# Instance norm over 512 rows: tiles of 48 KiB per partition in four slots, with parts of 16 KiB at both ends

## The chip, the core and the metric

The kernel runs on one core of one Trainium2 chip. The metric is device time in microseconds (us), from several runs of the whole program; before the change the median of 6 runs is 1248.16 us (1247.94 to 1249.8). One further run was recorded by the hardware profiler. PE is the matrix engine, DVE the vector engine, ACT the scalar engine, POOL the general engine that here only sets constants up, SP the engine that issues the loads. 16 DMA engines move data between HBM and the on-chip memory (128 partitions).

## What is computed

```python
def reference(x, eps):              # x: (8, 64, 32, 64, 64) float32
    mean = np.mean(x, axis=(2, 3, 4), keepdims=True)
    var = np.var(x, axis=(2, 3, 4), keepdims=True)
    return ((x - mean) / np.sqrt(var + eps)).astype(np.float32)
```

There are 8 x 64 = 512 instances of 32 x 64 x 64 = 131,072 floats. The input has 268.4 MB and the output as much; each is moved once.

## The kernel before

**Tiles and slots.** A tile is 128 partitions x 8,192 floats (32 KiB per partition, 4 MiB): 8 whole instances, each spread over 16 partitions. There are 64 tiles and six slots for them; tile k lives in slot k mod 6. Tiles 0 to 59 run in a loop of 10 rounds with six slots each (lines 168 to 173), tiles 60 to 62 behind it, and tile 63 as two halves of 4,096 columns side by side in one slot (lines 157 to 160), with lanes of their own. A lane is one set of semaphores and small columns.

**One tile.** ACT and DVE each sum half of the columns (lines 107 and 79). A matmul with a block-diagonal matrix holding 1/131072 (`avg`, line 136) adds up the 16 partitions of each instance, and DVE adds the two halves into the negative mean (line 82). ACT takes the square of x minus the mean over the whole tile with a running sum (line 113), a second matmul joins the partitions (line 143), ACT takes the root (line 120), and DVE the reciprocal and the shift (lines 89 and 92). Then ACT scales one half of the columns in place (line 123) and DVE the other (line 95).

**Queues.** SP issues all loads in order (lines 178 to 194): the first six at once, each later one when the store of the tile that last had its slot is complete (`stored`). ACT issues the stores (line 130) behind its own scaling, when both scalings are `done`. Both queues feed the same 16 DMA engines, 8 partitions of a transfer on each. Every engine works through the tiles in order, so the next tile's sums on ACT stand behind this tile's store. POOL prepares `avg` and `eps_t` (lines 196 to 215); PE and ACT wait for it once. ACT waits at the end for all stores.

Of the kernel before, what the change touches and what calls it, by code (L numbers as in the profile page):

```python
# [9 lines left out]
def kernel(  # L10
# [6 lines left out]
    nc = tc.nc  # L17
# [4 lines left out]
    P = 128  # L22
# [5 lines left out]
    COLS = 8192  # L28
    SLOTS = 6
    FULL = P * COLS // n_elem  # L30
    n_tiles = n_inst // FULL
    ROUNDS = (n_tiles - 1) // SLOTS
    LANES = SLOTS + 2

    x_f = x.rearrange("b c d h w -> (b c) (d h w)")
    out_f = out.rearrange("b c d h w -> (b c) (d h w)")
    x_t = x_f.rearrange("(k i) (s f) -> k (i s) f", i=FULL, s=P // FULL)
    out_t = out_f.rearrange("(k i) (s f) -> k (i s) f", i=FULL, s=P // FULL)
    x_h = x_f.rearrange("(k i) (s f) -> k (i s) f", i=FULL // 2, s=2 * P // FULL)
    out_h = out_f.rearrange("(k i) (s f) -> k (i s) f", i=FULL // 2, s=2 * P // FULL)  # L40

    ctx.enter_context(tc.tile_critical(name="norm"))  # L42

    def sbuf(name, shape, dtype=fp32):
# [4 lines left out]
    unused = sbuf("unused", [P, COLS], mybir.dt.uint8)  # L49
    eps_t = sbuf("eps_t", [P, 1])  # L50
    avg = {n: sbuf(f"avg{n}", [P, P]) for n in (FULL, FULL // 2)}
    small = [sbuf(f"small{i}", [P, 8]) for i in range(LANES)]
    psum = [
        ctx.enter_context(nc.psum_tensor(f"psum{i}", [P, 512], fp32))
        for i in range(LANES)
    ]

    def semaphores(name, n):
        return [ctx.enter_context(nc.semaphore(f"{name}{i}")) for i in range(n)]

    ready = semaphores("ready", 1)[0]
    landed = semaphores("landed", LANES)
    summed = semaphores("summed", LANES)
    meaned = semaphores("meaned", LANES)
    centred = semaphores("centred", LANES)
    squared = semaphores("squared", LANES)
    varied = semaphores("varied", LANES)
    rooted = semaphores("rooted", LANES)
    scaled = semaphores("scaled", LANES)
    shifted = semaphores("shifted", LANES)  # L70
    done = semaphores("done", LANES)
    stored = semaphores("stored", LANES)
# [3 lines left out]
    def on_vector(eng, t, lane, n, c1, c2, c16):  # L76
        w = t.shape[1] // 2
        a = small[lane]
        eng.reduce_sum(  # L79
            out=a[:, 0:1], in_=t[:, :w], axis=mybir.AxisListType.X  # L80
        )._wait_ge(landed[lane], c16).then_inc(summed[lane], 1)
        eng.tensor_reduce(  # L82
            out=a[:, 2:3],
            in_=psum[lane][:, 0:2],
            axis=mybir.AxisListType.X,
            op=Alu.add,
            negate=True,
        )._wait_ge(meaned[lane], c1).then_inc(centred[lane], 1)
        eng.reciprocal(out=a[:, 5:6], in_=a[:, 4:5])._wait_ge(  # L89
            rooted[lane], c1  # L90
        ).then_inc(scaled[lane], 1)
        eng.tensor_mul(out=a[:, 6:7], in0=a[:, 2:3], in1=a[:, 5:6])._wait_ge(  # L92
            scaled[lane], c1
        ).then_inc(shifted[lane], 1)
        eng.tensor_scalar(  # L95
            out=t[:, w:],
            in0=t[:, w:],
            scalar1=a[:, 5:6],
            scalar2=a[:, 6:7],
            op0=Alu.mult,  # L100
            op1=Alu.add,
        )._wait_ge(shifted[lane], c1).then_inc(done[lane], 1)

    def on_scalar(eng, t, lane, n, c1, c2, c16, dst):
        w = t.shape[1] // 2
        a = small[lane]
        eng.activation(  # L107
            out=unused[:, w : 2 * w],
            in_=t[:, w:],
            func=Act.Identity,  # L110
            accum_out=a[:, 1:2],
        )._wait_ge(landed[lane], c16).then_inc(summed[lane], 1)
        eng.activation(  # L113
            out=unused[:, : 2 * w],
# [4 lines left out]
        )._wait_ge(centred[lane], c1).then_inc(squared[lane], 1)  # L119
        eng.activation(  # L120
            out=a[:, 4:5], in_=psum[lane][:, 2:3], func=Act.Sqrt, bias=eps_t[:, 0:1]
        )._wait_ge(varied[lane], c1).then_inc(rooted[lane], 1)
# [4 lines left out]
            scale=a[:, 5:6],  # L127
            bias=a[:, 6:7],
        )._wait_ge(shifted[lane], c1).then_inc(done[lane], 1)
        eng.dma_start(out=dst, in_=t)._wait_ge(done[lane], c2).then_inc(  # L130
# [3 lines left out]
    def on_tensor(eng, t, lane, n, c1, c2, c16):  # L134
        a = small[lane]
        eng.matmul(  # L136
            out=psum[lane][:, 0:2],
            lhsT=avg[n][:],
            rhs=a[:, 0:2],
            start=True,  # L140
            stop=True,
        )._wait_ge(summed[lane], c2).then_inc(meaned[lane], 1)
        eng.matmul(  # L143
            out=psum[lane][:, 2:3],
            lhsT=avg[n][:],
            rhs=a[:, 3:4],
            start=True,
            stop=True,
        )._wait_ge(squared[lane], c1).then_inc(varied[lane], 1)


    rest = [
        (x_t[k], out_t[k], slots[k % SLOTS][:], k % SLOTS, k // SLOTS + 1, FULL)
        for k in range(ROUNDS * SLOTS, n_tiles - 1)
    ]
    last = (n_tiles - 1) % SLOTS
    for h in range(2):
        k = 2 * (n_tiles - 1) + h
        half = slots[last][:, h * COLS // 2 : (h + 1) * COLS // 2]
        rest.append((x_h[k], out_h[k], half, SLOTS + h, 1, FULL // 2))  # L160

    def over_tiles(eng, step, with_target=False):
        counts = [
            ctx.enter_context(eng.register(f"{step.__name__}_c{m}")) for m in (1, 2, 16)
        ]
        for c, m in zip(counts, (1, 2, 16)):
            eng.reg_mov(c, m)
        with eng.Fori(0, ROUNDS) as it:
            for s in range(SLOTS):
                more = (out_t[it * SLOTS + s],) if with_target else ()  # L170
                step(eng, slots[s][:], s, FULL, *counts, *more)
            for c, m in zip(counts, (1, 2, 16)):
                eng.reg_add(c, c, m)
        for _, dst, t, lane, c, n in rest:
            more = (dst,) if with_target else ()
            step(eng, t, lane, n, c, 2 * c, 16 * c, *more)

    def load_all(eng):
        for s in range(SLOTS):
            eng.dma_start(out=slots[s][:], in_=x_t[s]).then_inc(landed[s], 16)  # L180
# [8 lines left out]
        for src, _, t, lane, c, n in rest:  # L189
            behind = lane if lane < SLOTS else last  # L190
            uses = c - 1 if lane < SLOTS else ROUNDS
            eng.dma_start(out=t, in_=src)._wait_ge(stored[behind], 16 * uses).then_inc(
                landed[lane], 16
            )

    def set_up(eng):
        count = 0
        for n, m in avg.items():
            split = P // n

            eng.memset(m[:], 1.0 / n_elem).then_inc(ready, 1)  # L201
            count += 1
            for sign in (-1, 1):
                eng.affine_select(  # L204
                    out=m[:],
                    in_=m[:],
                    pattern=[[sign * split, n], [0, split]],
# [3 lines left out]
                    channel_multiplier=-sign,  # L211
# [53 lines left out]
```

## Time and profile before

| what | value |
|---|---|
| median of 6 runs | 1248.16 us (1247.94 to 1249.8) |
| the profiled execution, its own time | 1247.89 us |
| its span, first to last instruction | 1246.2 us |
| ACT busy | 986.0 us (79%), 410 instructions |
| DVE busy | 467.9 us (38%), 325 instructions |
| PE busy | 76.3 us (6%) |
| DMA | 18,722 packets, 536.90 MB, 431 GB/s over the span |
| loads, 4 MiB each: issue to landing | 53.3 us (median of 63) |
| stores, 4 MiB each: issue to landing | 45.3 us (median of 63) |

The span is what the instructions cover; the time is 1.69 us longer. A packet is one row of one transfer (one partition's contiguous bytes), or the 4-byte write behind each transfer's share on a DMA engine that counts up its semaphore. Busy shares are averages over the whole span.

### The profile page before, as it was taken

The numbers are of one execution on the slowest core, as the hardware profiler recorded it, in microseconds if no ns is written. First come the engines' busy times: TensorE is split into PE (matmuls) and PEld (weight loads), VectorE is DVE, ScalarE is ACT, GpSimd is POOL, SyncE is SP. The second block draws the span as 40 slices with busy tenths as digits, with TensorE's granted clock in tenths as the row PEclk, the third lists the DMA queues.
The fourth block names the chain that finished last, engine by engine and source line by source line (L and its number), as shares of the span: only waits on it lengthen the run. The fifth ranks groups of instructions, "written<-read, shape, count | busy, mean of one in ns | idle before, by whom it ended". The sixth has DMA issues, their size and how long they took to land.

```text
span 1246.2 us, 1808 instructions
## 1 busy us (share of the span) xinstructions
PE 76.3 (6%) x260; PEld 65.2 (5%) x260; DVE 467.9 (38%) x325; ACT 986.0 (79%) x410; POOL 1.9 (0%) x11
## 2 busy tenths in 40 slices
PE   0000000000000000000000000000000000000000
PEld 0000000000000000000000000000000000000000
DVE  2344334433334334343343433434334333343331
ACT  5888888887787878778777877787787778878774
POOL 0000000000000000000000000000000000000000
DMA  9999999999999999999999999999999999999998
GB/s 404 421 438 433 426 438 438 430 428 438 435 429 431 438 435 428 432 436 436 427 433 436 435 428 432 438 434 426 435 438 433 427 435 438 432 426 438 438 429 380
DMA packets 18722, 536.90 MB, mean 431 GB/s; under 512 B 2080, under 2 KB 2080, under 8 KB 2080
## 3 DMA queue, kind: packets, MB, share of 16 engines
q1 hardware_dynamic: 9360, 268.44, 50.0%
q10 hardware_dynamic: 9360, 268.44, 49.9%
q14 instruction: 2, 0.02, 0.0%
HBM read 268.44 MB, written 268.44 MB: 431 GB/s over the span
## 4 chain that ended last, share of the span: by engine, by line
ACT 48%; DVE 29%; another core or an unknown queue 13%; PE 6%; issue 1%; DMA 1%; ACTq 0%; DVEq 0%; SPq 0%
ACT unused L113 37%; DVE small L79 18%; DVE slot L95 8%; ACT slot L123 4%; ACT unused L107 4%; PE psum L136 3%; PE psum L143 3%; ACT small L120 1%; ACT L120 1%; DMA slot<-in_x_dram 1%; DVE small L89 1%; DVE small L82 1%; DVE small L92 1%; ACTq L130 0%
## 5 line engine op out<-in xcount | busy, mean ns | idle before, releaser
L113 ACT ACTIVATE unused<-slot,small 128x8192 uint8<-128x8192 f32 (+1 forms) x65 | 456.1, 7016 | 90.1 <-DVE small L82 90.1
L79 DVE TENSOR_REDUCE small<-slot 128x1 f32<-128x4096 f32 (+1 forms) x65 | 282.9, 4353 | 163.6 <-DMA slot<-in_x_dram 163.6
L107 ACT ACTIVATE unused<-slot 128x4096 uint8<-128x4096 f32 (+1 forms) x65 | 231.7, 3564 | 82.0 <-DMA slot<-in_x_dram 76.8
L123 ACT ACTIVATE slot<-slot,small 128x4096 f32<-128x4096 f32 (+1 forms) x65 | 243.7, 3749 | 27.6 <-DVE small L92 27.6
L89 DVE RECIPROCAL small<-small 128x1 f32<-128x1 f32 x65 | 10.6, 164 | 533.8 <-ACT small L120 533.8
L95 DVE TENSOR_SCALAR slot<-slot,small 128x4096 f32<-128x4096 f32 (+1 forms) x65 | 154.7, 2380 | 2.4
L136 PE MATMUL psum<-small,avg 128*128 128x2 f32 x130 | 38.1, 363 | 674.0 <-DVE small L79 548.5
L136 PEld LDWEIGHTS psum<-small,avg 128*128 128x128 f32 x130 | 32.6, 311 | 679.4 <-DVE small L79 552.8
L143 PE MATMUL psum<-small,avg 128*128 128x1 f32 x130 | 38.2, 363 | 480.5 <-ACT unused L113 480.5
L143 PEld LDWEIGHTS psum<-small,avg 128*128 128x128 f32 x130 | 32.6, 312 | 486.1 <-ACT unused L113 486.1
L120 ACT ACTIVATE small<-psum,eps_t 128x1 f32<-128x1 f32 x65 | 17.0, 261 | 37.3 <-PE psum L143 37.2
L82 DVE TENSOR_REDUCE small<-psum 128x1 f32<-128x2 f32 x65 | 10.3, 159 | 63.0 <-PE psum L136 63.0
L107 ACT ACT_TABLE_LOAD x10 | 12.8, 1283 | 10.4 <-ACT slot L123 7.1
L120 ACT ACT_TABLE_LOAD x10 | 12.8, 1283 | 0.2
L107 ACT ACTIVATION_READ_ACCUMULATOR unused<-slot 128x1 f32 x65 | 12.1, 186 | 0.0
L113 ACT ACTIVATION_READ_ACCUMULATOR unused<-slot,small 128x1 f32 x65 | 12.1, 186 | 0.0
L92 DVE TENSOR_TENSOR small<-small 128x1 f32<-128x1 f32 x65 | 10.3, 159 | 2.2
L204 POOL TENSOR_SCALAR_AFFINE_SELECT avg<-avg 128x128 f32<-128x128 f32 x4 | 1.3, 326 | 0.3
L201 POOL MEMSET avg<- 128x128 f32 x2 | 0.4, 206 | 0.5 <-SPq L42 0.5
L246 POOL MEMSET const-bfloat16-1.0<- 128x1 bf16 x1 | 0.1, 103 | 0.0
L246 POOL MEMSET const-uint8-127<- 128x1 uint8 x1 | 0.1, 102 | 0.0
L246 POOL MEMSET const-float32-0.0<- 128x1 f32 x1 | 0.1, 99 | 0.3 <-issue 0.3
(2 smaller groups left out, 0.2 us busy)
## 6 DMA issues: line engine op xcount, KB each, us to landing
slot<-in_x_dram SPq DMA_DIRECT2D x63, 4096.0 KB, 53.3
out_dram<-slot ACTq DMA_DIRECT2D x63, 4096.0 KB, 45.3
slot<-in_x_dram SPq DMA_DIRECT2D x2, 2048.0 KB, 55.6
out_dram<-slot ACTq DMA_DIRECT2D x2, 2048.0 KB, 14.7
```

The costliest lines, as they stand in the source:

```text
L79: eng.reduce_sum(out=a[:, 0:1], in_=t[:, :w], axis=mybir.AxisListType.X)._wait_ge(landed[lane], c16).then_inc(summed[lane], 1)
L82: eng.tensor_reduce(out=a[:, 2:3], in_=psum[lane][:, 0:2], axis=mybir.AxisListType.X, op=Alu.add, negate=True,)._wait_ge(meaned[lane], c1) ...
L89: eng.reciprocal(out=a[:, 5:6], in_=a[:, 4:5])._wait_ge(rooted[lane], c1).then_inc(scaled[lane], 1)
L92: eng.tensor_mul(out=a[:, 6:7], in0=a[:, 2:3], in1=a[:, 5:6])._wait_ge(scaled[lane], c1).then_inc(shifted[lane], 1)
L95: eng.tensor_scalar(out=t[:, w:], in0=t[:, w:], scalar1=a[:, 5:6], scalar2=a[:, 6:7], op0=Alu.mult, op1=Alu.add,)._wait_ge(shifted[lane], ...
L107: eng.activation(out=unused[:, w : 2 * w], in_=t[:, w:], func=Act.Identity, accum_out=a[:, 1:2],)._wait_ge(landed[lane], c16).then_inc(sum ...
L113: eng.activation(out=unused[:, : 2 * w], in_=t, func=Act.Square, bias=a[:, 2:3], accum_out=a[:, 3:4],)._wait_ge(centred[lane], c1).then_in ...
L120: eng.activation(out=a[:, 4:5], in_=psum[lane][:, 2:3], func=Act.Sqrt, bias=eps_t[:, 0:1])._wait_ge(varied[lane], c1).then_inc(rooted[lane ...
L123: eng.activation(out=t[:, :w], in_=t[:, :w], func=Act.Identity, scale=a[:, 5:6], bias=a[:, 6:7],)._wait_ge(shifted[lane], c1).then_inc(don ...
L136: eng.matmul(out=psum[lane][:, 0:2], lhsT=avg[n][:], rhs=a[:, 0:2], start=True, stop=True,)._wait_ge(summed[lane], c2).then_inc(meaned[lan ...
L143: eng.matmul(out=psum[lane][:, 2:3], lhsT=avg[n][:], rhs=a[:, 3:4], start=True, stop=True,)._wait_ge(squared[lane], c1).then_inc(varied[la ...
L204: eng.affine_select(out=m[:], in_=m[:], pattern=[[sign * split, n], [0, split]], compare_op=Alu.is_ge, fill=0.0, base=0 if sign < 0 else s ...
```

## The change

The data are cut anew, in address order: two parts of 4,096 columns (16 KiB per partition, 2 MiB, 4 instances), then 41 tiles of 12,288 columns (48 KiB per partition, 6 MiB, 12 instances), then three more parts. The whole tiles use four slots and 10 rounds of a loop plus tile 40. The first two parts lie in slots 2 and 3 and have lanes of their own, and the loads of tiles 2 and 3 wait for their stores. The last three parts lie side by side in slot 1, behind the store of tile 37.

A partition's 48 KiB can now hold the end of one instance and the start of the next, but each 16 KiB chunk belongs to one instance. So all sums are kept per chunk, spread with a 0/1 mask (`belongs`) to columns (instance class, chunk), joined by one matmul, added, and picked back per chunk with the mask (`over_instance`, twice per tile). DVE takes the sum of chunk 0 and of the last 1,536 columns, centres chunk 0 in place, takes its squares with a two-input instruction, and scales chunks 0 and 1; ACT takes the other sums, the squares of chunks 1 and 2, and scales chunk 2. The store of tile 40 is no longer issued by ACT: SP issues it on the load queue, behind the loads of the last three parts. SP, not ACT, waits for the last stores. POOL also builds the mask, DVE waits for POOL once, and ACT loads its function table ahead of its first wait.

The functions for the parts (`part_on_vector`, `part_on_scalar`, `part_on_tensor`, `part`) repeat the old steps on 4,096 columns, with constants in their waits. `over_tiles` runs parts 0 and 1, then the loop of 10 rounds, then tile 40 (where ACT gets no target and so issues no store), then parts 2 to 4. `CHUNK` is 4,096, so `n_tiles` is 41, `n_parts` 5 and `ROUNDS` 10.

```diff
-    COLS = 8192
-    SLOTS = 6
+    CHUNK = 4096
+    THIRDS = 3
+    COLS = THIRDS * CHUNK
+    SLOTS = 4
+    PART = P * CHUNK // n_elem
+    FRONT = 2
+    n_tiles = (n_inst // PART - FRONT) // THIRDS - 1
+    n_parts = n_inst // PART - THIRDS * n_tiles
+    ROUNDS = n_tiles // SLOTS
+    LANES = SLOTS + n_parts
...
+    within = sbuf("within", [P, PART * THIRDS, THIRDS])
+    TURN = 1536
+    belongs = sbuf("belongs", [P, THIRDS, THIRDS + 1])
...
+    SUMS, MEANS, SQUARES, VARS, ROOTS, SCALES, SHIFTS = 0, 28, 31, 55, 58, 61, 64
+    AXIS = mybir.AxisListType.X
+    def column(a, first, j):
+        return a[:, first + j : first + j + 1]
+    def block(a, first, n, m):
+        return a[:, first : first + n * m].rearrange("p (n m) -> p n m", m=m)
+    def spread(a, first, m):
+        return a[:, first : first + m].unsqueeze(1).to_broadcast([P, THIRDS, m])
+    def over_instance(eng, a, p, at, m, to, negate, c1, wait, steps):
+        n = THIRDS
+        by_both = at + m
+        by_instance = by_both + n * m
+        by_chunk = by_instance + n
+        eng.tensor_tensor(
+            out=block(a, by_both, n, m),
+            in0=spread(a, at, m),
+            in1=belongs[:, :, :m],
+            op=Alu.mult,
+        )._wait_ge(*wait).then_inc(steps[0], 1)
+        eng.tensor_reduce(
+            out=a[:, by_instance : by_instance + n],
+            in_=p.rearrange("p (n m) -> p n m", m=m),
+            axis=AXIS,
+            op=Alu.add,
+        )._wait_ge(steps[1], c1).then_inc(steps[2], 1)
+        eng.tensor_tensor(
+            out=block(a, by_chunk, n, n),
+            in0=spread(a, by_instance, n),
+            in1=belongs[:, :, :n].rearrange("p i c -> p c i"),
+            op=Alu.mult,
+        )._wait_ge(steps[2], c1).then_inc(steps[3], 1)
+        eng.tensor_reduce(
+            out=a[:, to : to + n],
+            in_=block(a, by_chunk, n, n),
+            axis=AXIS,
+            op=Alu.add,
+            negate=negate,
+        )._wait_ge(steps[3], c1).then_inc(steps[4], 1)
+    def tile_on_vector(eng, t, lane, c1, c3, c4, c16):
+        a, p = small[lane], psum[lane]
+        chunk = [t[:, i * CHUNK : (i + 1) * CHUNK] for i in range(THIRDS)]
+        for j, part in ((0, chunk[0]), (3, t[:, COLS - TURN :])):
+            eng.reduce_sum(out=column(a, SUMS, j), in_=part, axis=AXIS)._wait_ge(
+                landed[lane], c16
+            ).then_inc(summed[lane], 1)
+        over_instance(
+            eng, a, p[:, 0:12], SUMS, 4, MEANS, True, c1, (summed[lane], c4),
+            (sorted_[lane], meaned[lane], joined[lane], picked[lane], centred[lane]),
+        )
+        eng.tensor_scalar(
+            out=chunk[0],
+            in0=chunk[0],
+            scalar1=column(a, MEANS, 0),
+            scalar2=None,
+            op0=Alu.add,
+        )._wait_ge(centred[lane], c1).then_inc(moved[lane], 1)
+        eng.tensor_tensor_reduce(
+            out=unused[2][:],
+            in0=chunk[0],
+            in1=chunk[0],
+            scale=1.0,
+            scalar=0.0,
+            op0=Alu.mult,
+            op1=Alu.add,
+            accum_out=column(a, SQUARES, 0),
+        )._wait_ge(moved[lane], c1).then_inc(squared[lane], 1)
+        over_instance(
+            eng, a, p[:, 12:21], SQUARES, 3, VARS, False, c1, (squared[lane], c3),
+            (sorted2[lane], varied[lane], joined2[lane], picked2[lane], gathered[lane]),
+        )
+        eng.reciprocal(out=a[:, SCALES : SCALES + 3], in_=a[:, ROOTS : ROOTS + 3])._wait_ge(
+            rooted[lane], c1
+        ).then_inc(scaled[lane], 1)
+        eng.tensor_mul(
+            out=a[:, SHIFTS : SHIFTS + 3],
+            in0=a[:, MEANS : MEANS + 3],
+            in1=a[:, SCALES : SCALES + 3],
+        )._wait_ge(scaled[lane], c1).then_inc(shifted[lane], 1)
+        eng.tensor_scalar(
+            out=chunk[0],
+            in0=chunk[0],
+            scalar1=column(a, SCALES, 0),
+            scalar2=None,
+            op0=Alu.mult,
+        )._wait_ge(scaled[lane], c1).then_inc(done[lane], 1)
+        eng.tensor_scalar(
+            out=chunk[1],
+            in0=chunk[1],
+            scalar1=column(a, SCALES, 1),
+            scalar2=column(a, SHIFTS, 1),
+            op0=Alu.mult,
+            op1=Alu.add,
+        )._wait_ge(shifted[lane], c1).then_inc(done[lane], 1)
+    def tile_on_scalar(eng, t, lane, c1, c3, c4, c16, dst):
+        a = small[lane]
+        chunk = [t[:, i * CHUNK : (i + 1) * CHUNK] for i in range(THIRDS)]
+        for j, part in ((1, chunk[1]), (2, chunk[2][:, : CHUNK - TURN])):
+            eng.activation(
+                out=unused[j - 1][:, : part.shape[1]],
+                in_=part,
+                func=Act.Identity,
+                accum_out=column(a, SUMS, j),
+            )._wait_ge(landed[lane], c16).then_inc(summed[lane], 1)
+        for j in (1, 2):
+            eng.activation(
+                out=unused[j - 1][:],
+                in_=chunk[j],
+                func=Act.Square,
+                bias=column(a, MEANS, j),
+                accum_out=column(a, SQUARES, j),
+            )._wait_ge(centred[lane], c1).then_inc(squared[lane], 1)
+        eng.activation(
+            out=a[:, ROOTS : ROOTS + 3],
+            in_=a[:, VARS : VARS + 3],
+            func=Act.Sqrt,
+            bias=eps_t[:, 0:1],
+        )._wait_ge(gathered[lane], c1).then_inc(rooted[lane], 1)
+        eng.activation(
+            out=chunk[2],
+            in_=chunk[2],
+            func=Act.Identity,
+            scale=column(a, SCALES, 2),
+            bias=column(a, SHIFTS, 2),
+        )._wait_ge(shifted[lane], c1).then_inc(done[lane], 1)
+        if dst is not None:
+            eng.dma_start(out=dst, in_=t)._wait_ge(done[lane], c3).then_inc(
+                stored[lane], 16
+            )
+    def tile_on_tensor(eng, t, lane, c1, c3, c4, c16):
+        a, p = small[lane], psum[lane]
+        for at, m, col, before, after in (
+            (SUMS, 4, 0, sorted_, meaned),
+            (SQUARES, 3, 12, sorted2, varied),
+        ):
+            eng.matmul(
+                out=p[:, col : col + THIRDS * m],
+                lhsT=avg[PART][:],
+                rhs=a[:, at + m : at + m + THIRDS * m],
+                start=True,
+                stop=True,
+            )._wait_ge(before[lane], c1).then_inc(after[lane], 1)
...
+    TAIL = n_tiles - 1
...
     def load_all(eng):
+        def part(m):
+            lane, t, slot, uses = parts[m]
+            load = eng.dma_start(out=t, in_=part_of(x_f, m))
+            if uses:
+                load._wait_ge(stored[slot], 16 * uses)
+            load.then_inc(landed[lane], 16)
+        for m in range(FRONT):
+            part(m)
+        for s in range(SLOTS):
+            load = eng.dma_start(out=slots[s][:], in_=x_t[s])
+            if s >= SLOTS - FRONT:
+                load._wait_ge(stored[s + FRONT], 16)
+            load.then_inc(landed[s], 16)
...
+        for k in range(ROUNDS * SLOTS, n_tiles):
+            eng.dma_start(out=slots[k % SLOTS][:], in_=x_t[k])._wait_ge(
+                stored[k % SLOTS], 16 * (k // SLOTS)
+            ).then_inc(landed[k % SLOTS], 16)
+        for m in range(FRONT, n_parts):
+            part(m)
+        s = TAIL % SLOTS
+        eng.dma_start(out=out_t[TAIL], in_=slots[s][:])._wait_ge(
+            done[s], 3 * (TAIL // SLOTS + 1)
+        ).then_inc(stored[s], 16)
+        for s in range(SLOTS):
+            eng.wait_ge(stored[s], 16 * len(range(s, n_tiles, SLOTS)))
+        for m in range(FRONT, n_parts):
+            eng.wait_ge(stored[SLOTS + m], 16)
...
+    nc.vector.wait_ge(ready, set_by)
+    nc.scalar.preload_act_table(Act.Sqrt)
```

## The prediction

> **What bounds the kernel now.** I read the page first: the slices of the span, the DMA queues, then the groups by line.
>
> ```profile
> DMA  9999999999999999999999999999999999999998
> GB/s 404 421 438 433 426 438 438 430 428 438 435 429 431 438 435 428 432 436 436 427 433 436 435 428 432 438 434 426 435 438 433 427 435 438 432 426 438 438 429 380
> DMA packets 18722, 536.90 MB, mean 431 GB/s; under 512 B 2080, under 2 KB 2080, under 8 KB 2080
> ...
> q14 instruction: 2, 0.02, 0.0%
> ...
> L113 ACT ACTIVATE unused<-slot,small 128x8192 uint8<-128x8192 f32 (+1 forms) x65 | 456.1, 7016 | 90.1 <-DVE small L82 90.1
> L79 DVE TENSOR_REDUCE small<-slot 128x1 f32<-128x4096 f32 (+1 forms) x65 | 282.9, 4353 | 163.6 <-DMA slot<-in_x_dram 163.6
> ```
>
> The DMA row is 9 from end to end; the engines' first sums (L79) wait for landings. The chain that ended last gives ACT 48%, but it steps through whatever waited last: ACT idles 1.7 us before a tile until it lands. **The 16 DMA engines are the bound.** Next I asked for the DMA queues in three windows: 600 to 1100 (rows of 32 KiB only), 1236 to 1241 (16 KiB only) and 1196 to 1216 (loads of 16 KiB beside stores of 32 KiB).
>
> ```profile
> DMA packets 7443, 216.83 MB, mean 434 GB/s; under 512 B 826, under 2 KB 826, under 8 KB 826
> ...
> q10 hardware_dynamic: 3722, 108.53, 50.3%
> q1 hardware_dynamic: 3721, 108.30, 50.2%
> ```
>
> ```profile
> DMA packets 149, 2.18 MB, mean 436 GB/s; under 512 B 16, under 2 KB 16, under 8 KB 16
> ...
> q10 hardware_dynamic: 149, 2.18, 101.8%
> ```
>
> ```profile
> q10 hardware_dynamic: 193, 5.73, 66.4%
> q1 hardware_dynamic: 193, 2.90, 33.8%
> ```
>
> The last pair shows turns taken packet by packet: equal counts, so the larger rows get the larger share. The others give the price of a packet. 100.5% of 16 engines over 500 us is 8040 us for 6617 rows of 32 KiB and 826 four-byte packets; 101.8% of 80 us is 81.4 us for 133 rows of 16 KiB and 16 small ones. The single records behind it say 1213 ns (15,795 of 16,128), 611 ns (506 of 512) and 9 ns. So **602 ns per 16 KiB and 9 ns per packet**; successive packets on an engine overlap by 3.5 ns in the records, so a packet costs 5.5 ns beyond its bytes. Bytes alone: 2048 x 0.602 = 1232.9 us per engine; 18,720/16 = 1170 packets x 5.5 ns = 6.4 us; some 1.4 us go to the first load and the first store, whose packets last about 0.6 us longer. The sum of 1240.7 us, from the first packet at 2.1, is 1242.8. The end by windows of 1 us (columns: stretch, length, then PE, PEld, DVE, ACT, POOL busy, clock, DMA share, GB/s):
>
> ```profile
> 1242.00:1243.00 1.00, 0.00 (x0) 0.00 (x0) 0.00 (x0) 0.00 (x0) 0.00 (x0) 1.00 0.69 295
> 1243.00:1244.00 1.00, 0.00 (x0) 0.00 (x0) 0.00 (x0) 0.00 (x0) 0.00 (x0) 1.00 0.04 16
> 1244.00:1245.00 1.00, 0.00 (x0) 0.00 (x0) 0.00 (x0) 0.00 (x0) 0.00 (x0) 1.00 0.04 16
> ```
>
> Most engines are done near 1242.8; one works alone until 1244.6. It is the one that carried both instruction packets of q14 (309 ns each, and the packets behind them were 113 and 351 ns longer: 1.1 us). 1.6 us of final waits close the span.
>
> So an arrangement that moves the same bytes can win at most 6.4 + 1.4 + 1.8 (the lone engine) = 9.6 us, 0.8%. The Trainium skill, "DMA: Bandwidth & Descriptors", section "Where 436 GB/s comes from", puts the ceiling at 435.2 GB/s; by it the bytes need 1233.6 us, which would leave 7.1 us of the 1240.7, where the packet rows leave 7.8.
>
> **The change, part by part.**
>
> *Larger rows.* Before, 1040 rows and 130 counting packets per engine. After: 41 tiles x 16 + 5 parts x 16 = 736 rows and 46 x 2 = 92 counting packets, 828 together. 342 fewer x 5.5 ns = **1.9 us saved**. No row of the trace has 48 KiB; if the overlap is nearer to the 5 ns that the window's 0.5% gives, a packet costs 4 ns or less (1.0 us saved at 3 ns), and if it costs its whole 9 ns, 3.1 us. I take 5.5 ns, from the most records.
>
> *Compute per tile*, as it must stay below the DMA's period of 16 x (3 x 0.602 + 0.0055) + 0.01 = 29.0 us. Sums: ACT 3.62 (L107, 4096) + 2.34 (2560, between 1.91 for 2048 and 3.62) + two reads of the accumulator, 6.2; DVE 4.42 + 1.75 (1536, on the slope of 2.28 and 4.42), 6.2. Mask, matmul, add, mask, add: four small DVE steps at 0.19 with their gaps and the matmul at 0.63 (L136 to L82): 1.4. Squares: ACT 2 x 3.8 = 7.6; DVE 2.41 to centre (L95's row) and the two-input instruction, which no row shows: between 2.4 (L95) and 8.8 (twice the 4.42 of L79), I take 4.4 as it too reads through a sum; 7.0 with gaps, so ACT is later. Second join 1.4, root, reciprocal and shift 0.7, then two scalings on DVE, 4.9 (ACT's one, 3.8, beside them). Sum **22.2 us** and 0.4 for the store's issue: 6.4 us of slack per tile. Even 8.8 makes it 26. So the masked sums, some eight small instructions per tile and the in-place centring cost nothing, hidden by the DMA's period.
>
> *Added waits.* ACT's store now waits 1.1 us for DVE's second scaling, with the next tile's sums behind it; counted above. DVE's wait for POOL: set-up grows from 11 to 15 instructions, done by 4 us against 2.99; the first part lands near 8.5 (13.3 before, less 8 x 0.6). ACT's table loads (20 x 1.28 us) fall to one; they were hidden.
>
> *The front.* Loads of parts 0, 1 and tiles 0, 1 are queued at once: 9.7 + 29 = 38.7 us of work, so the DMA engines run alone on loads as before (six tiles of 9.7 then). Part 0's store is issued near 19 (8.5 + 10.2, the 1212.1 to 1222.3 of the half tile). SP then waits for it, with tiles 2, 3 and all later loads behind. Its rows of 16 KiB take turns with 48 KiB: 8 x 2.4 = 19 us, and some 4 us lead as at the first store before (31.66 issued, first packets past 36): done near 43, when the load queue still has some 4 us and part 1's store follows. No gap: 0 us. Cover gone, each us late costs 1 us.
>
> *The end.* When tile 40 lands (call it T), tile 37 has been stored for about 20 us (116 us per slot, less 22.6, shared in the ratio 53.3 to 45.3 of loads and stores before). Left for the DMA besides the last part's store: a rest of tile 38's, 4 to 8 us; tiles 39 and 40, 14.5 each; three loads 14.6; two stores 9.7: 57 to 61 us. The last part's store can start at T + 22.2 + 3 x 10.4 + issue and start, 2.3 = T + 56. So it arrives 1 to 5 us before the queues run dry. That holds because tile 40's store goes out on SP's queue, where nothing but the final waits stands behind it, and shares the engines with the parts' stores. Cost 0; if the last store is late, up to its own 4.9 us.
>
> Sum: 1247.89 - 1.9 = 1246.0 for the profiled execution; the median of the runs lies 0.3 higher, so the forecast for it is **1246.3 us** (-0.15%). About 0.2% is what a measurement of this kernel can tell from no change; that is 2.5 us, the border at 1245.7.
>
> **Rivals.**
>
> 1. *More saved*: 9 ns per packet (-3.1) and no lone engine at the end (-1.1): 1244.0. For it: the 9 ns are in every record. Against: the overlap is too. 9%.
> 2. *The end runs dry*: the last part's store is late by some 2 us: 1248.3 (no change), at most 1251. For it: a margin of 1 us at worst, and three parts in a row with 10.4 us each against 4.9 of DMA. Against: before's two halves ended in the same order, and its DMA row keeps 9 into the last slice but one. 9%.
> 3. *Rows of 48 KiB are split* by the queue: in 32 + 16, 1484 packets per engine, +314 x 5.5 ns: 1249.9; in three of 16, 2140 packets, +5.3: 1253.5, slower. For it: no such row was seen. Against: 32 KiB go out whole. 3% each. [...]
> 4. *Slower, by instruction fetch*: DVE's loop has 60 instructions per round where it had 30. If it no longer stays in the engine, each of 10 rounds brings a packet on one DMA engine at 0.54 us, the mean of the two above: +5.4, 1251.7; decisive from eight fetches on. Against: ACT and DVE fetched nothing per round, two packets in all. 5%.
> 5. *DVE becomes the bound*: if the two-input instruction takes over 11.4 us (6.4 of slack + the 5.0 at which DVE's squares would end with ACT's), 41 tiles pay each us more: at 13.3 (three passes of L79) 1.9 x 41 = 78, 1324. 3%.
>
> **Numbers.** My own case has 68%, 1244.1 to 1248.2 (saving 1.0 to 3.1, and the lone engine up to 1 us shorter or longer); a third of it lies under 1245.7. Faster: 0.23 + 0.09 = 0.32. Same: 0.45 + 0.07 (rival 2) + 0.03 (split in two) = 0.55. Slower: 0.02 (rival 2 at worst) + 0.03 (split in three) + 0.05 + 0.03 = 0.13. The range 1244.0 to 1249.0 takes in rivals 1 and 2 but for the worst of 2, and leaves 3 to 5 out (0.14).
>
> **What would show it.** 13,248 packets of the two data queues instead of 18,720; rows of 48 KiB at 1815 ns; a tile every 29.0 us with DVE and ACT waiting about 6 us for landings; DMA at 9 throughout. Wrong if slices before the last fall below 9, if packets exceed 20,000, if L173 takes over 11 us, or if q14 has ten packets.

## The result, and the profile after

The changed kernel takes 1251.76 us (median of 16 runs, 1247.35 to 1253.85) against 1248.08 (median of 37 runs of the kernel before). The ratio is 1.0022, with a 95% interval of 1.0015 to 1.0028 (by the means of the runs; the medians give 1.0029): **slower by 0.2%**, where 1246.3 and a range of 1244.0 to 1249.0 were forecast. The 16 runs fall into two groups: five at 1247.35 to 1248.79, eleven at 1251.65 to 1253.85. The profiled execution, 1248.47 us with a span of 1246.8, belongs to the lower group. Three runs of two of the copies below took 1436 to 1449 us, some 15% more than all others of the same kernels, and are left out.

The page after, lines that answer those of before:

```profile
DMA  9999999999999999999999999999999999999998
GB/s 395 429 429 440 438 431 431 429 438 435 435 429 432 437 437 432 432 431 435 438 434 431 431 437 438 434 431 431 432 442 435 431 431 432 442 432 434 434 422 361
DMA packets 13250, 536.89 MB, mean 431 GB/s; under 512 B 1472, under 2 KB 1472, under 8 KB 1472
...
q14 instruction: 2, 0.02, 0.0%
...
L159 DVE TENSOR_REDUCE small<-slot 128x1 f32<-128x4096 f32 x82 | 249.2, 3081 | 273.0 <-DMA slot<-in_x_dram 273.0
...
L173 DVE CUSTOM_DVE_ANT_0 unused<-slot 128x4096 uint8<-128x4096 f32 x41 | 181.4, 4425 | 1.4
```

Packets fell from 18,722 to 13,250, as counted; DMA is 9 throughout; the two-input instruction (L173) takes 4.43 us; q14 still has two packets. The same DMA window as before, 600 to 1100:

```profile
DMA packets 4957, 216.91 MB, mean 434 GB/s; under 512 B 544, under 2 KB 544, under 8 KB 544
...
q10 hardware_dynamic: 2479, 108.48, 50.1%
q1 hardware_dynamic: 2478, 108.43, 50.1%
```

100.2% of 8000 us, less 544 small packets, is 8011 us for 4413 rows: 1815 ns each, the forecast 9 + 3 x 602. The Trainium skill, "DMA: Bandwidth & Descriptors", section "Why a DMA increments its semaphore by 16 and not by 1", says that one descriptor moves one contiguous run of the last dimension; the count and this duration agree with that for rows of 48 KiB.

So far all is as forecast. In this execution the loss stands at the very end (columns as in the windows of before):

```profile
1240.00:1241.00 1.00, 0.00 (x0) 0.00 (x0) 0.00 (x0) 0.00 (x0) 0.00 (x0) 1.00 1.07 459
1241.00:1242.00 1.00, 0.00 (x0) 0.00 (x0) 0.00 (x0) 0.00 (x0) 0.00 (x0) 1.00 0.43 180
1242.00:1243.00 1.00, 0.00 (x0) 0.00 (x0) 0.00 (x0) 0.00 (x0) 0.00 (x0) 1.00 0.31 131
1243.00:1244.00 1.00, 0.00 (x0) 0.00 (x0) 0.00 (x0) 0.00 (x0) 0.00 (x0) 1.00 0.31 131
1244.00:1245.00 1.00, 0.00 (x0) 0.00 (x0) 0.00 (x0) 0.00 (x0) 0.00 (x0) 1.00 0.04 16
```

A share of 0.31 is five of 16 engines. Eleven are done at 1241.1 to 1241.9, five work on until 1244.0 to 1245.0. The median engine ends at 1241.6 where it ended at 1242.9 before: 1.3 us won. The last one ends at 1245.0 where it ended at 1244.6: all of it given back. A transfer's share is fixed, 8 partitions to each engine, so an engine that falls behind is not helped by the others, and the last store waits for it. The single records show how they fell behind: not idle, but by packets that last longer. In the window 1206 to 1214, where the last part is loaded while stores of 48 KiB have just ended, 16 KiB rows of these five take up to 1.3 us instead of 611 ns.

That is less than half of it. Summed over the 16 engines, the packets from 1172 us on, where rows of 16 KiB come beside rows of 48 KiB, last 7.2 us longer than 611 and 1815 ns each would make. From 70 to 1172 us, where both queues hold rows of 48 KiB only, they last 8.9 us longer, 7.3 of it in loads and 0.8 right behind instruction packets. In the kernel before the same two sums are 0.5 and 1.8 us.

### The profile page after: what moved, and what is told of

Its sections match the earlier page's. It is cut to its first block, busy times and chain, and to the rows that moved or that the text cites. A ratio compares the mean times of both kernels' runs of the same rounds, so it can differ in the third digit from the quotient of the medians.

```text
span 1246.8 us, 1977 instructions
## 1 busy us (share of the span) xinstructions
PE 55.0 (4%) x184; PEld 46.1 (4%) x184; DVE 804.4 (65%) x722; ACT 764.5 (61%) x441; POOL 2.7 (0%) x15
## 2 busy tenths in 40 slices
DMA packets 13250, 536.89 MB, mean 431 GB/s; under 512 B 1472, under 2 KB 1472, under 8 KB 1472
## 4 chain that ended last, share of the span: by engine, by line
another core or an unknown queue 82%; DMA 8%; ACT 5%; DVE 2%; SPq 1%; issue 1%; PE 1%; ACTq 0%
DMA slot<-in_x_dram 4%; DMA out_dram<-slot 4%; ACT unused L292 1%; ACT unused L222 1%; SPq L389 1%; ACT unused L215 1%; ACT slot L302 1%; DVE slot L202 0%; DVE small L266 0%; DVE slot L195 0%; ACT unused L289 0%; PE psum L253 0%; PE psum L315 0%; PE psum L318 0%
## 5 line engine op out<-in xcount | busy, mean ns | idle before, releaser
L215 ACT ACTIVATE unused<-slot 128x4096 uint8<-128x4096 f32 x82 | 243.3, 2968 | 303.1 <-DMA slot<-in_x_dram 300.8
L159 DVE TENSOR_REDUCE small<-slot 128x1 f32<-128x4096 f32 x82 | 249.2, 3081 | 273.0 <-DMA slot<-in_x_dram 273.0
L222 ACT ACTIVATE unused<-slot,small 128x4096 uint8<-128x4096 f32 x82 | 303.4, 3701 | 63.6 <-DVE small L145 63.6
L173 DVE CUSTOM_DVE_ANT_0 unused<-slot 128x4096 uint8<-128x4096 f32 x41 | 181.4, 4425 | 1.4
L235 ACT ACTIVATE slot<-slot,small 128x4096 f32<-128x4096 f32 x41 | 155.9, 3801 | 18.0 <-DVE small L190 18.0
L202 DVE TENSOR_SCALAR slot<-slot,small 128x4096 f32<-128x4096 f32 x41 | 98.7, 2406 | 0.0
L253 PE MATMUL psum<-small,avg 128*128 128x9 f32 (+1 forms) x164 | 49.1, 375 | 1116.9 <-DVE small L127 1116.9
L166 DVE TENSOR_SCALAR slot<-slot,small 128x4096 f32<-128x4096 f32 x41 | 96.5, 2353 | 1.5
L195 DVE TENSOR_SCALAR slot<-slot,small 128x4096 f32<-128x4096 f32 x41 | 96.2, 2346 | 0.0
L253 PEld LDWEIGHTS psum<-small,avg 128*128 128x128 f32 x164 | 41.1, 311 | 1124.9 <-DVE small L127 1124.9
L127 DVE TENSOR_TENSOR small<-small,belongs 128x12 f32<-128x12 f32 x82 | 13.9, 169 | 31.2 <-ACT unused L222 28.9
L292 ACT ACTIVATE unused<-slot,small 128x4096 uint8<-128x4096 f32 x5 | 18.5, 3707 | 6.0 <-DVE small L269 6.0
L139 DVE TENSOR_TENSOR small<-small,belongs 128x9 f32<-128x9 f32 x82 | 13.9, 170 | 2.8
L215 ACT ACTIVATION_READ_ACCUMULATOR unused<-slot 128x1 f32 x82 | 15.3, 186 | 0.0
```

The costliest lines, as they stand in the source:

```text
L127: eng.tensor_tensor(out=block(a, by_both, n, m), in0=spread(a, at, m), in1=belongs[:, :, :m], op=Alu.mult,)._wait_ge(*wait).then_inc(steps ...
L139: eng.tensor_tensor(out=block(a, by_chunk, n, n), in0=spread(a, by_instance, n), in1=belongs[:, :, :n].rearrange("p i c -> p c i"), op=Alu ...
L159: eng.reduce_sum(out=column(a, SUMS, j), in_=part, axis=AXIS)._wait_ge(landed[lane], c16).then_inc(summed[lane], 1)
L166: eng.tensor_scalar(out=chunk[0], in0=chunk[0], scalar1=column(a, MEANS, 0), scalar2=None, op0=Alu.add,)._wait_ge(centred[lane], c1).then_ ...
L173: eng.tensor_tensor_reduce(out=unused[2][:], in0=chunk[0], in1=chunk[0], scale=1.0, scalar=0.0, op0=Alu.mult, op1=Alu.add, accum_out=colum ...
L195: eng.tensor_scalar(out=chunk[0], in0=chunk[0], scalar1=column(a, SCALES, 0), scalar2=None, op0=Alu.mult,)._wait_ge(scaled[lane], c1).then ...
```

## The experiments

Each ran beside the kernel before on one chip, but not all on the same one; the median of the kernel before was 1248.04 to 1248.09 us on each. Times are those of the single runs; "engine ends" come from the 16 four-byte packets behind the last store in the profile's DMA records. A copy is a kernel with the DMAs alone, without arithmetic.

**1. The changed kernel again, and three edits.** `r1_same` is unaltered. `r2_tail_on_act` undoes the place of tile 40's store (excerpts, here and below):

```diff
-            if with_target and k == TAIL:
-                more = (None,)
...
-        eng.dma_start(out=out_t[TAIL], in_=slots[s][:])._wait_ge(
-            done[s], 3 * (TAIL // SLOTS + 1)
-        ).then_inc(stored[s], 16)
```

`r3_copy48` and `r4_copy32` keep the DMAs of the two kernels and drop the arithmetic; a store then waits only for its landing:

```diff
+    def copy_tile(eng, t, lane, c1, c3, c4, c16, dst):
+        if dst is not None:
+            eng.dma_start(out=dst, in_=t)._wait_ge(landed[lane], c16).then_inc(stored[lane], 16)
...
-    over_tiles(nc.vector, part_on_vector, tile_on_vector)
-    over_tiles(nc.tensor, part_on_tensor, tile_on_tensor)
-    over_tiles(nc.scalar, part_on_scalar, tile_on_scalar, with_target=True)
+    over_tiles(nc.scalar, copy_part, copy_tile, with_target=True)
```

> The changed kernel, unaltered. Its runs so far fall into two groups, 1247.35 to 1248.79 (the profiled one is among them) and 1251.65 to 1253.85. In the profile 11 DMA engines end near 1241.2 to 1241.9 us, as forecast, and five near 1244.0 to 1245.0. Theory A (memory conflicts): the two groups differ by how far single DMA engines fall behind through packets that last longer than 611 or 1815 ns; a profile at 1252 would show engines ending near 1248 with lengthened packets, and no hole while others work. Theory B (a hole at the end): a profile at 1252 shows a stretch after 1230 in which most DMA engines have nothing to do, because the last part's store is late. Theory C (rows of 48 KiB are dearer): the tile period is over 29.05 us in a profile at 1252, where the profile at 1248.5 has 29.05. Time expected by all three: about 1252 in most runs, 1248 in some.

> Only the place of tile 40's store is undone: ACT issues it behind its own scaling, ahead of the last parts. By the count of the prediction the store then stands ahead of the last parts' stores in one queue while the load queue is empty. Theory A: the DMA still has work until the last part's store, which is issued near 1232, but the order of stores changes: the queue runs dry about 4 us before that store, so about +4 (1252 from 1248, or 1256 from 1252). Theory B: if a hole at the end is the loss already, it grows by the same 4 us or less. Theory C: no change, as the rows are the same.

> Left out: all arithmetic, so the output is the input. The same loads and stores as the changed kernel, each store issued as soon as its tile has landed. Rows of 48 KiB, five parts of 16 KiB. Theory A: two groups or a spread of 1 to 4 us remain, with some DMA engines late by lengthened packets; mean engine work 1238.8 us, time 1245 to 1250. Theory B: no compute, so no late store: 1244 to 1246 in all runs, no spread. Theory C: over 1250 in all runs.

> Left out: all arithmetic, so the output is the input. The loads and stores of the kernel before, rows of 32 KiB, two half tiles at the end. All theories: about 1246 to 1248, without a second group. Theory A and B expect the copy with rows of 48 KiB to have 1.9 us less of mean engine work than this one; Theory C expects this one to be faster by 3 us or more.

| run | us | ratio to before (95%) | median engine, last engine end |
|---|---|---|---|
| r1_same | profiled 1249.2; 1252.06, 1252.37, 1253.18 | 1.0029 (1.0015 to 1.0043) | 1241.5, 1245.9 |
| r2_tail_on_act | 1256.40 to 1258.89 | 1.0075 (1.006 to 1.0089) | 1255.5, 1255.5 |
| r3_copy48 | profiled 1246.07; 1250.20, 1252.51 | 1.0012 (0.9991 to 1.0033) | 1241.5, 1242.7 |
| r4_copy32 | 1246.99 to 1247.52 | 0.9993 (0.9979 to 1.0007) | 1243.5, 1244.0 |

The profile of r1 has the same end as the first: most engines done by 1241.8, four late, the last at 1245.9:

```profile
1242.00:1243.00 1.00, 0.00 (x0) 0.00 (x0) 0.00 (x0) 0.00 (x0) 0.00 (x0) 1.00 0.31 131
1243.00:1244.00 1.00, 0.00 (x0) 0.00 (x0) 0.00 (x0) 0.00 (x0) 0.00 (x0) 1.00 0.19 82
1244.00:1245.00 1.00, 0.00 (x0) 0.00 (x0) 0.00 (x0) 0.00 (x0) 0.00 (x0) 1.00 0.08 33
1245.00:1246.00 1.00, 0.00 (x0) 0.00 (x0) 0.00 (x0) 0.00 (x0) 0.00 (x0) 1.00 0.04 16
```

r2 shows what a hole looks like:

```profile
1238.00:1242.00 4.00, 0.50 (x2) 0.50 (x2) 2.29 (x1) 2.00 (x2) 0.00 (x0) 1.00 0.23 98
1242.00:1246.00 4.00, 0.09 (x1) 0.00 (x0) 0.16 (x1) 3.68 (x2) 0.00 (x0) 1.00 0.06 25
1246.00:1250.00 4.00, 0.59 (x2) 0.50 (x2) 1.67 (x3) 2.48 (x4) 0.00 (x0) 1.00 0.01 4
1250.00:1255.00 5.00, 0.00 (x0) 0.00 (x0) 0.00 (x0) 0.00 (x0) 0.00 (x0) 1.00 0.99 419
```

Shares of 0.23, 0.06 and 0.01 while DVE and ACT still work on the last part, then all 16 engines together at 0.99: the store came late. The changed kernel has nothing of that kind, so SP's store of tile 40 is worth about 5 us and the forecast's "cost 0" for the end held. Theory B fails: the copy has no late store and still spreads by 6 us. Theory C, as a fixed price of the rows, fails: the median engine of r3 ends 2.0 us before that of r4, where 1.9 were expected, and r3 has a run at 1246.07. The tile period is 29.07 us in the first profile (L215 starts at 1148.03 and 1177.10); in a run at 1252 it was not seen. In r1 the two sums of lengthening, from 1172 us and before, are 4.5 and 7.8 us. What r3 has and r4 has not is the spread. No profile fell in the group at 1252, so that it comes from engines that are still further behind is inferred, not seen.

**2. Which transfers make it.** Copies again. Whole tiles move in three transfers of 4,096 columns instead of one, for loads and stores (r5), stores alone (r6), loads alone (r7); r8 has whole rows and no parts at the front (42 tiles, then two parts).

```diff
-            load = eng.dma_start(out=slots[s][:], in_=x_t[s])
...
+        for i in range(n):
+            d = eng.dma_start(out=out[:, i * w : (i + 1) * w], in_=in_[:, i * w : (i + 1) * w])
```

> Left out: all arithmetic, so the output is the input. As the copy with rows of 48 KiB, but each whole tile is loaded and stored by three transfers of 4,096 columns, so every packet has 16 KiB; addresses, slots and order stay. By the packet price of 5.5 ns: 2296 packets per engine instead of 828, +8.1, about 1252 to 1254. Theory A with the conflict in the long rows: no spread between runs, all within 1 us, near 1253. Theory A with the conflict in the addresses (48 KiB pitch, shifted tiles): spread of some us remains, 1253 to 1259.

> Left out: all arithmetic, so the output is the input. Only the stores of the whole tiles go out in three transfers of 16 KiB rows; loads keep 48 KiB. Price: 734 packets more per engine, +4.0, about 1248.5 to 1250 if nothing else happens. If long rows of stores are what spreads the runs, this one has no spread; if long rows of loads are, it has one of 3 us or more, up to 1254.

> Left out: all arithmetic, so the output is the input. The mirror: loads of whole tiles in three transfers of 16 KiB rows, stores keep 48 KiB. Price +4.0, about 1248.5 to 1250. If long rows of loads spread the runs, no spread here; if long rows of stores do, 3 us or more of spread.

> Left out: all arithmetic, so the output is the input. Rows of 48 KiB in 42 tiles, no parts at the front and two at the end, so tile addresses are no longer shifted by 4 MiB. If the shift or the front parts cause the spread: all runs near 1245 to 1246. If the rows of 48 KiB do: 1246 to 1253 as in the copy with front parts.

r5: 1252.71 to 1254.41, as the packet price says: 1134 packets per engine more than r4 for 6.9 us of median, 6.1 ns each. r6: **1294.18 to 1297.58**, and r7: **1272.96 to 1283.04**, where both were priced at 1248.5 to 1250. r8: nine of eleven runs at 1245.91 to 1247.24, two at 1249.6 (one of them the profiled one); ratio 0.9987 (0.9978 to 0.9996).

Neither "long loads" nor "long stores" explains this, since r6 and r7 are both far worse than all-long and all-short. What they share is that **the two queues hold packets of different size all the time**. The page of r6, and of r6 and r5 one line each for the window 600 to 1100:

```profile
GB/s 390 431 432 431 424 427 415 428 427 434 418 438 418 427 422 432 428 429 425 425 428 432 425 425 423 426 430 428 420 426 427 423 429 429 434 413 420 373 419 58
DMA packets 25056, 536.88 MB, mean 415 GB/s; under 512 B 2784, under 2 KB 2784, under 8 KB 2784
...
DMA packets 9991, 213.24 MB, mean 426 GB/s; under 512 B 1124, under 2 KB 1124, under 8 KB 1124
...
DMA packets 14795, 215.67 MB, mean 431 GB/s; under 512 B 1632, under 2 KB 1632, under 8 KB 1632
```

Two things are lost: a little rate everywhere (426 GB/s in that window where r5 has 431), and the last slice at 58 GB/s, in which one engine works alone from 1267 to 1292. In the records 23.5% of the 48 KiB loads last over 20 ns longer than the 1815; all packets together last 19.6 us per engine longer than nominal. In r7 it is 4.9% of the 16 KiB loads and 20.4 us in all; in r5 0.4% and 1.7 us, nearly all in the first transfers. Theory A took a new form: with unequal packets the engines run out of step and hold one another's loads up. That unequal packets cost this much, in lengthened packets, is what these runs show; how it comes about is not shown.

**3. The new form tested in the full computation.** r9 takes the parts at the front away (`FRONT = 0`, 42 tiles, two parts at the end). r10 also stores its last three whole tiles in three transfers each, so that 16 KiB stands against 16 KiB there. r11 is the kernel before with only its loads halved, 16 KiB against stores of 32 KiB. r12 is a copy with parts at the front alone. The edit of r11:

```diff
+        w = COLS // 2
+        for i in range(2):
+            d = eng.dma_start(out=out[:, i * w : (i + 1) * w], in_=in_[:, i * w : (i + 1) * w])
...
-        for c, m in zip(counts, (1, 2, 16)):
+        for c, m in zip(counts, (1, 2, 32)):
```

> Full computation; the changed kernel without parts at the front: 42 tiles of 48 KiB from the start, two parts of 16 KiB at the end. 792 packets per engine and queue pair instead of 828 or 1170. Theory A, by now in the form 'while packets of different size stand on the two queues, the 16 DMA engines run out of step and delay single load packets; the slowest engine sets the end': no unequal sizes until about 1175 us, so no group at 1252, all runs at 1246 to 1249, where only the end differs. Rival D (rows of 48 KiB are fickle by themselves, whatever stands beside them): the group at 1252 remains.

> Full computation. As the run without parts at the front, and the stores of the last three whole tiles go out as three transfers of 16 KiB rows each, so that beside the two parts all packets have 16 KiB: equal sizes on both queues from start to end, but for some us at the change. Theory A: 324 packets fewer than before at 5.5 to 6 ns, 1.8 to 1.9 us saved, 1246.0 to 1246.6 in nearly all runs, faster than both kernels. Rival D: no better than the run without parts at the front, and 0.3 us dearer by its packets.

> Full computation; the kernel before, with only this changed: each whole tile is loaded by two transfers of 4,096 columns, so loads have packets of 16 KiB and stores of 32 KiB all through. By the packet price alone: 567 packets more per engine, +3.3, 1251.4 in all runs. Theory A: the unequal sizes cost more than the price: 1255 to 1285, spread of some us, many lengthened packets, one or two engines far behind. Rival D: 1251.4.

> Left out: all arithmetic, so the output is the input. The copy with rows of 48 KiB, two parts of 16 KiB at the front and 42 tiles, no parts at the end. Theory A: unequal sizes only while the first parts are stored, some 40 us; after that the engines keep whatever phases they got. If that is enough for the slower group, some runs at 1249 to 1253 as in the copy with parts at both ends; if the end is what does it, all runs at 1245 to 1247. Rival D: a spread in either case, also in the copy without front parts, which had 9 of 11 runs within 1245.9 to 1247.3.

r11: 1281.45 to 1287.77, ratio 1.0294 (1.0278 to 1.0311), 37 us where the packet price is 3.3. Its page and the window 600 to 1100:

```profile
GB/s 394 430 420 425 425 430 417 429 421 421 427 419 422 424 421 424 419 427 424 423 420 429 421 423 425 424 430 414 418 430 424 424 427 426 416 424 426 420 400 270
DMA packets 27794, 536.90 MB, mean 418 GB/s; under 512 B 3088, under 2 KB 3088, under 8 KB 3088
```

```profile
q1 hardware_dynamic: 7347, 106.96, 51.5%
q10 hardware_dynamic: 3600, 104.86, 49.0%
```

The same engine share as before, 100.5%, moves 212 MB in 500 us instead of 217: packets last longer, the engines are not idle. The records put it at 25.4 us per engine. The rest of the 37 us, beyond these and the 3.3, lies in a hole near the end (shares of 0.60 from 1250 to 1260 and 0.31 from 1270 to 1278), which the late loads bring as in r2; behind it all 16 engines end within 0.2 us, at 1282.1. That unequal packets cost dearly when they last is shown, in the kernel before too.

r12 has three of ten runs at 1249.3 to 1251.7, the rest at 1245.1 to 1248.0. That does not show that the front parts, some 40 us of unequal packets, bring the spread: r8 without them has two of eleven runs at 1249.6, on another chip. In r12's profile the engine that ends last, 2.8 us behind the median, has 2.0 us of its delay in five loads of 48 KiB from 107 to 312 us, when no small row was left.

But r9 and r10 did **not** do what theory A said. r9: 1247.96 to 1253.67, median 1249.82, ratio 1.0017 (1.0008 to 1.0026). r10, with equal packets nearly throughout, was expected at 1246.0 to 1246.6 and took 1248.24 to 1258.31, median 1249.64, ratio 1.0019 (1.0006 to 1.0032). Two groups no longer stand apart, but three of twelve runs lie above 1251.4 in each. The medians are 2 us better than the changed kernel's, the means less than 1 us, and the intervals of the ratios overlap: a gain is not shown, and the spread stays. The end of r10:

```profile
1241.00:1242.00 1.00, 0.00 (x0) 0.00 (x0) 0.00 (x0) 0.00 (x0) 0.00 (x0) 1.00 0.81 344
1242.00:1243.00 1.00, 0.00 (x0) 0.00 (x0) 0.00 (x0) 0.00 (x0) 0.00 (x0) 1.00 0.15 66
1243.00:1244.00 1.00, 0.00 (x0) 0.00 (x0) 0.00 (x0) 0.00 (x0) 0.00 (x0) 1.00 0.12 49
1244.00:1246.00 2.00, 0.00 (x0) 0.00 (x0) 0.00 (x0) 0.00 (x0) 0.00 (x0) 1.00 0.04 16
```

One engine alone again, until 1245.6. Its records have loads lengthened by 59 to 261 ns at 1119.8, 1149.1 and 1178.4, one tile period apart; another engine had them at 198.7, 227.7, 256.9, 315.0, 373.2 and 402.5. An engine that has slipped is met at the same place of every tile. So rival D is right for this part: tiles of 48 KiB rows are fickle without any unequal packet. r8's profiled run had the same at 1246.4 for one engine. The 8.9 us in the loop of the changed kernel are of this kind.

**4. Length or addresses.** Bare copies of whole tiles, all built alike, varying the row and the distance at which rows start in HBM:

```diff
+    COLS = 12288
+    PITCH = 16384
...
+        rows = flat[: n_tiles * P * PITCH].rearrange("(k p f) -> k p f", p=P, f=PITCH)
+        return rows[:, :, :COLS]
```

> Left out: all arithmetic, and a quarter of the data: 32 tiles of rows of 48 KiB that lie back to back. Work per engine 32 x 29.0 = 928, time about 932 to 934. Both theories (addresses, length): some runs or the profile show single engines 1 to 4 us behind, by lengthened load packets.

> Left out: all arithmetic, and a quarter of the data: 32 tiles of rows of 48 KiB that start every 64 KiB. Work 928, about 932. If the addresses do it: all runs within 0.5 us and no engine more than 1 us behind but by an instruction packet. If the length of the packet does it: the same spread as with rows back to back.

> Left out: all arithmetic, and a third of the data: 42 tiles of rows of 32 KiB that start every 48 KiB. Work 42 x 19.37 = 813.5, about 818. If the addresses do it: spread of 1 us or more and single engines behind, though the packets are as short as before. If the length does it: none, as with rows of 32 KiB back to back.

> Left out: all arithmetic and the last third of a tile: 85 tiles of rows of 24 KiB back to back, eight slots. Work 85 x 14.54 = 1236, about 1240. If addresses that are no power of two apart do it: spread and single engines behind. If packets longer than 32 KiB do it: none, within 0.5 us.

> Left out: all arithmetic, and a quarter of the data: 64 tiles of rows of 24 KiB that start every 32 KiB, eight slots. Work 64 x 14.55 = 931, about 935. If the distance of row starts decides (bad above 32 KiB): all runs within 1 us, no engine more than 1.5 us behind. If holes between rows decide: a spread of 2 us or more.

> Left out: all arithmetic, and half of the data: 32 tiles of rows of 32 KiB that start every 64 KiB, six slots. Work 32 x 19.37 = 620, about 624. If the distance decides, or if holes do: a spread of 2 us or more and single engines behind. If rows 48 KiB apart are a case of their own: all runs within 1 us.

| rows, start to start | runs | spread | last engine behind the median one |
|---|---|---|---|
| 48 KiB, 48 (r13) | 936.26 to 940.39 | 4.1 | 0.7 us |
| 48 KiB, 64 (r14) | 935.60 to 937.97 | 2.4 | 2.3 us |
| 32 KiB, 48 (r15) | 821.56 to 830.38 | 8.8 | 2.3 us |
| 24 KiB, 24 (r16) | 1243.84 to 1244.68 | 0.8 | 1.1 us |
| 24 KiB, 32 (r17) | 937.98 to 938.09 | 0.1 | 0.4 us |
| 32 KiB, 64 (r18) | 626.89 to 627.46 | 0.6 | 0.9 us |

In r15 the last column says too little. The last store waits for the last load, and that is late on single engines while the others stand idle (columns: stretch, length, POOL busy, clock, DMA share, GB/s):

```profile
808.00:812.00 4.00, 0.00 (x0) 1.00 0.29 123
812.00:816.00 4.00, 0.00 (x0) 1.00 0.36 156
816.00:820.00 4.00, 0.00 (x0) 1.00 0.94 401
```

No simple rule survives. Length alone fails, since rows of 32 KiB that start every 48 spread most. Addresses alone do not explain it, since 48 KiB rows every 64 spread too. Holes between rows do not explain it (r17 and r18 are steady), nor does a start distance above 32 KiB (r18), but this is weaker: r17 and r18 ran on another chip than r13 to r16, and r18 for 627 us only. Every unsteady case has 48 KiB in it, as length or as distance. With four or five runs each that is as far as it goes: the kernel before, with rows of 32 KiB, has two of 37 runs at 1249.8 and 1250.3 too, and r14's spread is no larger than that. The number of slots changed with the row (4, 6 or 8) and was not varied alone; r15 and r18 both have six. **Why** stays open.

No version with the full computation beat the kernel before.

## Why the prediction was wrong

- **The step that failed** is the end of the sum: "the lone engine up to 1 us shorter or longer". The forecast took the 16 engines as one server, by their mean work, and moved the last engine with the mean. That term was +1.7 and +2.6 us in the two profiles of the changed kernel (last engine 3.5 and 4.4 us behind the median one, where it was 1.8 before). Eleven of 16 runs are about 3 to 5 us longer than the profiled one; that this is the same term, grown, is inferred. What the profiles show in its place are lengthened packets, more than half of it while both queues hold rows of 48 KiB, the rest where 16 KiB stand beside 48. Why they last longer stays open.
- **The reason for the 1.8 us** was misread, too. When each packet is given to the engine whose last one ended 3.5 ns after its start, the instruction packets at 107.5 and 1191.9 us lie on two engines that end at 1243.2 and 1243.4. A third, without one, ends at 1244.6, slowed by many packets that last some 10 ns longer. So the lone engine of before was already late by lengthened packets, and the forecast, which put 1.1 us of it down to instruction packets, had no term for them.
- **The row saving** was right: 1.9 us forecast, 2.0 by the median engine of the two copies, 1.3 by that of the full kernels (1.5 by the eight engines that end first, which the late five do not touch).
- **Turns packet by packet** were read rightly from the window 1196 to 1216, and used only for the time of part 0's store (SP issued tile 2's load near 42.9, forecast 43). That the same window showed unequal packets without harm was taken as no cost. There it was only 32 KiB against 16 KiB for some 30 us at the end, with 15 engines that end within 0.8 us of one another; r11 shows 37 us when it lasts.
- **Compute per tile** was right: from first sum to store 1148.03 to 1169.92, 21.9 us against 22.2; ACT waits 7.7 us per tile for landings, where about 6 were forecast. (DVE's loop has 64 instructions per round, 16 per tile, not the 60 of rival 4; with two packets on q14 it changes nothing.)
- **Front and end** had no hole, so "cost 0" held for both. Part 0 lands at 8.8 (8.5), its store is issued at 19.3 (19), the last part's store at 1231.7, 54.6 us after tile 40 landed (56, with its start).
- None of the rivals happened: the lone engine did not vanish (rival 1), and there was no hole, no split rows, two packets on q14, L173 at 4.43 us. The forecast had no rival in which the mean gets better and the last engine worse, though the windows of before already showed that the last engine, not the mean, ends the kernel.

## What to carry to other kernels

When the DMA engines are the bound, count for each engine, not for their mean: look at the last microseconds by windows, where a share of 0.04 to 0.07 is one engine of 16 working alone. Keep the packets on the load and the store queue of one size wherever both run side by side for long; what a short stretch of unequal packets at an end costs is not settled here, as r9 and r10 do not differ. A saving of 0.15% is less than what a row size can add in spread, so compare many runs, not one profile.

## What the runs showed of the hardware

- A row of 16, 24, 32 or 48 KiB is one packet, at 602 ns per 16 KiB and 9 ns; successive packets overlap by 3.5 ns. By r5 against r4 a packet costs 6.1 ns beyond its bytes.
- Unequal packets on the two queues all the time (16 KiB against 32 or 48: r6, r7, r11) lengthen mostly loads: 20 to 25 us per engine over the kernel, and 27 to 48 us more time than the kernel before.
- Rows of 48 KiB, or rows of 32 KiB that start every 48, gave runs that differ by 2 to 10 us, with single DMA engines late; 24 and 32 KiB rows at 24, 32 and 64 KiB differed by 0.8 us at most in four or five runs each, though the kernel before, at 32, differs by 2.4 in 37. No run here tells the cause.
